# Hybrid encoder step, one core: low parts of the 128x1024 weight chunks formed by a casting and an accumulating DMA

## Chip, core and metric

The kernel runs on one NeuronCore of a Trainium2 chip. The metric is the device time of one execution, in microseconds. Three runs of the kernel before gave 2122.63, 2123.02 and 2124.85 us; the median is 2123.02 us. Five engines work side by side, each through its own queue in program order: PE (TensorE, matrix products), DVE (VectorE), ACT (ScalarE), POOL (GpSimd) and SP (SyncE, which here only issues DMAs). DMAs that POOL issues have their descriptors written by POOL itself (the software queue q0 of the profile); those of SP go through the hardware queue q1.

## What is computed

Two layers of a hybrid encoder trunk over 640 token rows (512 of a prompt, 8 x 16 of decode streams). Cut to what matters:

```python
for l in range(2):
    h = rmsnorm(x)
    a_x, a_b, a_c, dq, dk, dv, fq, fk, fv, ff, pu = split(h @ w_in[l])     # 1024 -> 2308 columns
    o_a, o_b, o_c, o_d = conv(...), diff_attn(...), fox_attn(...), pool_mix(...)
    merged = sum(sigmoid(h @ w_gate[l, i] + b) * (o_i @ w_branch[l, i]) for i in range(4))
    x = x + rmsnorm(merged @ w_out[l])
    gu = rmsnorm(x) @ w_ffn_in[l]                                          # 1024 -> 2 * 2816
    x = x + rmsnorm((silu(gu[:2816]) * gu[2816:]) @ w_ffn_out[l])
```

All of it is float32. Every matrix product is made of three products of rounded operands: each operand is split into a high part (`hi`, rounded to float32r) and a low part (`lo` = operand - `hi`), and the product is hi x hi + hi x lo + lo x hi.

## The kernel before

**Weights in chunks.** All weights come through one list, `chunks`, in the order in which they are used. A chunk is 128 rows by at most 1032 columns; its kind says how it is prepared. Kind "n" (lines 234 to 250) is the ordinary one: the chunk is loaded by SP into a tile `raw` (two buffers, line 260), and then split in halves of 512 (516) columns, the `subs`: for each half ACT copies the half into `whi` with rounding (line 295, by `copy`, line 117) and DVE subtracts it from `raw` into `wlo` (line 274, in `flush`). `whi` and `wlo` have four buffers of 516 columns each. Chunks of kind "n" with more than 512 columns are 72 in each layer: 16 of w_in and 4 of w_v, 24 of w_gate, 4 of w_out, 6 of w_ffn_in, 18 of w_ffn_out. The other kinds: "x" chunks are split as a whole into tiles that stay, "r" chunks are only loaded, and "s" parts are sums of weight blocks (the Strassen stages), which pass through the same `whi` and `wlo`; the w_branch chunks are "n" with 512 or 256 columns.

**Who drives it.** A stage asks for a half with `w_sub(key, p)` (line 310): the half is split if it was not yet, the waiting subtractions are issued (`flush`), and `w_ahead` (line 302) splits two halves more. `w_done` starts the load of the next chunk but one once a chunk's last subtraction has been issued. The order is written out by hand (`manual_schedule`): every engine's queue has the order of the Python calls, and a later instruction of an engine cannot pass an earlier one that waits.

**Stages of a layer** (times of layer 0; layer 1 follows some 1048 us later with the same shape): the first two w_in chunks in `ab_start` (line 392; to 36 us), the other chunks of the input projection in `p0` and `p1a` (lines 1367 and 1379; each chunk is 8 k-steps of 6 matmuls, `dense_k`), the gates and branches of two phases (line 1399; to 494 us) with the attention units woven in by `drive`, a Strassen stage for the last gate (to 563 us), the output projection (`mix_phase`, line 1620), `ab_start` again for the first two w_ffn_in chunks, four more of those (to 675 us), 19 Strassen steps of 7 products (line 1843, `product` at line 1831; to 913 us), and `mix_phase` for w_ffn_out.

**What the prediction's steps touch.** In `ab_start` the third chunk is asked for by `w_ahead(keys[1], 1)`, after the second half of the first chunk's products and after its evacuation:

```python
        for i in range(2):
            dense(Ds[i], w[i], x, (1,))
            evac_fn(i, Ds[i])
            if i == 0:
                w_ahead(keys[1], 1)
```

For w_in the evacuation is `ev_pu` (line 1100), which issues on POOL a memset and then the store `out_pool` (line 1111), which waits for DVE copies of the evacuated tile. POOL also carries `rstd_of` (line 338), the low parts of the attention caches (lines 746 and 758, in the decode units), the weight sums of the Strassen stages (line 451) and five small stores.

## Time and profile before

| | us |
|---|---|
| median of three runs | 2123.02 |
| span of the profiled execution | 2121.1 |
| PE busy in it | 2044.4 |
| DVE busy | 1489.7 |
| ACT busy | 983.7 |
| POOL busy | 694.6 |

The profiled execution lies 1.9 us below the median of the runs; the terms of a sum are made against its span. PE is granted its full clock nearly throughout. A busy share is an average over stages; the lists of waits say in which stage an engine stood still and for whom. A group of instructions is named by line, engine, operation and tiles (`wlo<-raw,whi`); "[2.23 <-DVE wlo L274]" behind a row of a timeline is the idle time before it and what ended it. For a DMA the issue is a row of the issuing engine, and "to landing" the time from that issue to the last byte.

### The profile page before, as it was taken

What the parts mean: (1) busy time and instruction counts of PE and PEld (TensorE: products, weight loads), DVE (VectorE), ACT (ScalarE), POOL (GpSimd) and SP (SyncE); (2) the same over time, 40 slices, a digit from 0 to 9 for tenths busy, and PEclk for the clock granted to TensorE, in tenths of its full rate; (3) what the DMA queues carried; (4) which work ended last, traced back from release to release, by engine and by line L of the source; (5) the groups of instructions that cost most, each with busy time, mean ns of one, the idle gap of its engine ahead of it and who ended that gap; (6) DMA issues with size and microseconds to landing.
All of it is one profiled execution on the core that took longest, in us unless ns stands there. A gap on an engine that the chain in (4) does not pass through costs nothing.

```text
span 2121.1 us, 34713 instructions
## 1 busy us (share of the span) xinstructions
PE 2044.4 (96%) x13050; PEld 1927.9 (91%) x13050; DVE 1489.7 (70%) x2746; ACT 983.7 (46%) x2100; POOL 694.6 (33%) x618
## 2 busy tenths in 40 slices
PE   7999999989999999999999999999899999999998
PEld 7999999988889999988899999999888899999887
DVE  5677477689768888853475774775996698888432
ACT  5556455545443433443356554565444444334431
POOL 3111055465315444400040101554751345543000
PEclk9999999999999999999999999999999999999999
DMA  4312244332251222222523122443223422222223
GB/s 146 108 61 86 72 145 138 124 123 75 94 172 60 80 81 91 89 80 75 169 75 117 57 82 82 152 149 130 83 72 115 159 75 80 80 88 67 92 97 119
DMA packets 100744, 214.35 MB, mean 101 GB/s; under 512 B 10896, under 2 KB 35056, under 8 KB 100576
## 3 DMA queue, kind: packets, MB, share of 16 engines
q1 hardware_dynamic: 99552, 209.16, 29.6%
q0 software_dynamic: 1024, 2.98, 0.4%
q8 instruction: 102, 1.67, 0.3%
q14 instruction: 66, 0.54, 0.1%
HBM read 196.02 MB, written 16.08 MB: 100 GB/s over the span
## 4 chain that ended last, share of the span: by engine, by line
PE 68%; DVE 18%; issue 6%; ACT 3%; DMA 2%; POOL 2%; SPq 0%; DVEq 0%; ACTq 0%; POOLq 0%
PE D L376 21%; PE D L1632 11%; PE S L1837 7%; DVE wlo L274 6%; PE D L1837 4%; PE O L1632 3%; PE T L1632 3%; PE D L1413 2%; DVE s L1849 2%; PE T L1837 2%; PE O L1837 2%; PE D L1274 2%; DVE s L473 1%; PE O L808 1%; ACT whi L117 1%
## 5 line engine op out<-in xcount | busy, mean ns | idle before, releaser
L274 DVE TENSOR_TENSOR wlo<-raw,whi 128x512 fp32r<-128x512 f32 (+2 forms) x388 | 294.6, 764 | 183.1 <-ACT whi L117 178.7
L117 ACT ACTIVATE whi<-raw 128x512 fp32r<-128x512 f32 (+2 forms) x390 | 230.3, 606 | 166.9 <-issue 73.8
L274 DVE TENSOR_TENSOR wlo<-s,whi 128x512 fp32r<-128x512 f32 x196 | 210.7, 1077 | 17.9 <-ACT whi L117 16.6
L117 ACT ACTIVATE s<-s 128x512 fp32r<-128x512 f32 (+7 forms) x294 | 176.3, 619 | 91.7 <-POOL s L1425 38.7
L376 PE MATMUL D<-Qh,whi 128*128 128x320 f32 (+2 forms) x736 | 177.1, 315 | 4.0 <-DVE s L1417 3.6
L376 PE MATMUL D<-Ph,whi 128*128 128x320 f32 (+2 forms) x736 | 176.8, 314 | 4.2 <-DVE s L1417 3.5
L338 POOL TENSOR_TENSOR r<-ms,mhalf 128x1 f32<-128x1 f32 x40 | 22.0, 551 | 477.1 <-DVE ms L1677 408.5
L376 PE MATMUL D<-Qh,wlo 128*128 128x320 f32 (+2 forms) x736 | 174.3, 311 | 3.8 <-DVE wlo L274 3.8
L376 PE MATMUL D<-Ph,wlo 128*128 128x320 f32 (+2 forms) x736 | 173.8, 310 | 4.3 <-DVE wlo L274 4.3
L376 PE MATMUL D<-Ql,whi 128*128 128x320 f32 (+2 forms) x736 | 173.8, 310 | 0.0
L376 PE MATMUL D<-Pl,whi 128*128 128x320 f32 (+2 forms) x736 | 173.4, 310 | 0.0
L746 POOL TENSOR_TENSOR s<-s,s 128x512 fp32r<-128x512 f32 x64 | 85.0, 1328 | 181.9 <-ACT s L117 168.9
L117 ACT ACTIVATE whi<-s 128x512 fp32r<-128x512 f32 x196 | 117.3, 621 | 36.4 <-PE S L1837 12.4
L758 POOL TENSOR_TENSOR s<-s,s 128x512 fp32r<-128x512 f32 x64 | 92.9, 1469 | 123.0 <-ACT s L117 100.9
L376 PEld LDWEIGHTS D<-Qh,whi 128*128 128x128 f32 x736 | 123.5, 190 | 6.8 <-DVE s L1417 4.4
L376 PEld LDWEIGHTS D<-Qh,wlo 128*128 128x128 f32 x736 | 125.2, 189 | 4.6 <-DVE wlo L274 4.6
L376 PEld LDWEIGHTS D<-Ph,wlo 128*128 128x128 f32 x736 | 124.5, 189 | 5.3 <-DVE wlo L274 5.3
L376 PEld LDWEIGHTS D<-Ph,whi 128*128 128x128 f32 x736 | 123.0, 189 | 7.0 <-DVE s L1417 4.0
L376 PEld LDWEIGHTS D<-Ql,whi 128*128 128x128 f32 x736 | 125.6, 189 | 0.2
L376 PEld LDWEIGHTS D<-Pl,whi 128*128 128x128 f32 x736 | 125.1, 189 | 0.6 <-DVE Pl L120 0.4
L451 POOL TENSOR_TENSOR s<-V,V 128x512 f32<-128x512 f32 x48 | 77.1, 1607 | 94.4 <-DMA V<-in_w_fi 67.0
L117 ACT ACTIVATE s<-T 128x320 fp32r<-128x320 f32 (+6 forms) x132 | 50.9, 386 | 99.1 <-PE T L520 61.5
(487 smaller groups left out, 5978.9 us busy)
## 6 DMA issues: line engine op xcount, KB each, us to landing
raw<-in_w_gate SPq DMA_DIRECT2D x48, 512.0 KB, 3.5
raw<-in_w_fi SPq DMA_DIRECT2D x48, 512.0 KB, 3.5
raw<-in_w_fo SPq DMA_DIRECT2D x44, 512.0 KB, 3.5
V<-in_w_fi SPq DMA_DIRECT2D x80, 256.0 KB, 3.0
raw<-in_w_in SPq DMA_DIRECT2D x32, 512.0 KB, 3.4
s<-in_ck_d SPq DMA_DIRECT2D x32, 256.0 KB, 4.3
s<-in_cv_d SPq DMA_DIRECT2D x32, 256.0 KB, 4.0
s<-in_ck_f SPq DMA_DIRECT2D x32, 256.0 KB, 4.1
```

The source lines that it names most:

```text
L117: A.activation(out=out, in_=in_, func=AF.Copy, scale=scale)
L274: E.tensor_tensor(out=lo, in0=raw, in1=hi, op=ALU.subtract)
L338: G.tensor_tensor(out=out, in0=ssum, in1=mhalf[:, :n], op=ALU.pow)
L376: PE.matmul(Dt[:, h, :c1 - c0], a, b[:, k, c0:c1], start=(start and pi == 0), stop=(stop and pi == 2))
L451: G.tensor_tensor(out=o[:, :512], in0=x, in1=y, op=op)
L746: G.tensor_tensor(out=lo[:, :512], in0=raw[:, :512], in1=f32(hi[:, :512]), op=ALU.subtract)
L758: G.tensor_tensor(out=lo[:, :512], in0=t[:, :512], in1=f32(hi[:, :512]), op=ALU.subtract)
L1274: PE.matmul(acc[t], x, w[:, kk, :], start=(k == 0 and pi == 0), stop=(k == 7 and pi == 2))
L1413: PE.matmul(Dt[:, h, :HT], w[:, b, k, :], x[:, 2 * br + k, h * HT:(h + 1) * HT], start=(c == 0), stop=(c == 5))
L1632: PE.matmul(ps, a, b, start=(first and pi == 0), stop=(last and pi == 2))
L1837: PE.matmul(ps[:, :HT], w, x[k], start=(k == 0 and pi == 0), stop=(k == 3 and pi == 2))
L1849: V.tensor_tensor(out=out, in0=a, in1=b, op=op)
```

## The change

Chunks of kind "n" with more than 512 columns get a kind of their own, "a", and leave the list of SP loads. Such a chunk takes a pair of tiles `whi` and `wlo` of 1032 columns (three buffers each; before, four of 516), and three steps make it: POOL issues a DMA from DRAM that casts the chunk into `whi`; ACT writes -`whi` into `wlo` (128x1024); POOL issues a second DMA from the same place in DRAM that adds the chunk onto `wlo`. The steps are moved on by `w_step`, which is called in every `w_sub` and at a few other places; an entry goes one step further per call, and all the way when the asked-for half is its own. `w_ahead` now looks at most two pairs ahead of the current one. The remaining users of `whi` and `wlo` take halves of such pairs (`w_half`). At the start, the first two chunks are asked for before the loads of x for tiles 3 and 4, and the two subtractions that POOL did there (`flush(G)`) are gone. The scratch space for POOL's DMA descriptors is set to 8192 bytes per partition.

```diff
--- before.py
+++ after.py
@@ -241,13 +241,16 @@
                 sidx[key, p] = len(subs)
                 subs.append((key, p, i, 0, 512, kind, False))
             continue
+        if kind == "n" and n > 512:
+            for p in range(2):
+                sidx[key, p] = len(subs)
+                subs.append((key, p, i, p * (n // 2), n // 2, "a", p == 1))
+            continue
         loads.append(i)
         if kind == "r":
             continue
-        parts = 2 if kind == "n" and n > 512 else 1
-        for p in range(parts):
-            sidx[key, p] = len(subs)
-            subs.append((key, p, i, p * (n // parts), n // parts, kind, p == parts - 1))
+        sidx[key, 0] = len(subs)
+        subs.append((key, 0, i, 0, n, kind, True))
     lpos = {i: n for n, i in enumerate(loads)}
     raw_t, hl_t = {}, {}
     ptr = {"dma": 0, "split": 0}
@@ -257,7 +260,7 @@
         while ptr["dma"] <= min(upto, len(loads) - 1):
             i = loads[ptr["dma"]]
             _, src, n, _ = chunks[i]
-            t = wpool.tile([128, 1032], F32, tag="raw", name=nm("raw"))
+            t = wpool.tile([128, 1024], F32, tag="raw", name=nm("raw"))
             SP.dma_start(out=t[:, :n], in_=src)
             raw_t[i] = t
             ptr["dma"] += 1
@@ -267,6 +270,9 @@
         w_dma(lpos[i] + 2)
 
     low_part = []
+    pipe = []
+    calls = [0]
+    half = []
 
     def flush(E=V):
         while low_part:
@@ -275,10 +281,41 @@
             if done:
                 done()
 
+    def w_step(j=-1):
+        calls[0] += 1
+        for e in list(pipe):
+            must = e["j"] <= j
+            if e["stage"] == 0 and (must or e["call"] < calls[0]):
+                copy(e["lo"], f32(e["hi"]), -1.0)
+                e["stage"], e["call"] = 1, calls[0]
+            if e["stage"] == 1 and (must or e["call"] < calls[0]):
+                G.dma_start(out=e["lo"], in_=e["src"], accum_op=ALU.add)
+                pipe.remove(e)
+
+    def w_pair():
+        return tuple(wpool.tile([128, 1032], F32R, tag=t, bufs=3, name=nm(t)) for t in ("whi", "wlo"))
+
+    def w_half():
+        if not half:
+            pair = w_pair()
+            half.extend([[t[:, c:c + 512] for t in pair] for c in (0, 512)])
+        return half.pop(0)
+
     def w_split(upto):
         while ptr["split"] <= min(upto, len(subs) - 1):
             j = ptr["split"]
             key, p, i, off, n, kind, end = subs[j]
+            ptr["split"] += 1
+            if kind == "a":
+                if p == 0:
+                    half.clear()
+                    hi, lo = w_pair()
+                    src = chunks[i][1]
+                    G.dma_start(out=hi[:, :2 * n], in_=src)
+                    pipe.append({"j": j, "hi": hi[:, :2 * n], "lo": lo[:, :2 * n], "src": src, "stage": 0, "call": calls[0]})
+                    for q in range(2):
+                        hl_t[j + q] = (hi[:, q * n:(q + 1) * n], lo[:, q * n:(q + 1) * n])
+                continue
             if kind == "s":
                 src, done = ext[key[0]](key, p)
             else:
@@ -292,25 +329,36 @@
                 flush()
                 w_done(i)
             else:
-                hi = wpool.tile([128, 516], F32R, tag="whi", bufs=4, name=nm("whi"))
-                lo = wpool.tile([128, 516], F32R, tag="wlo", bufs=4, name=nm("wlo"))
+                hi, lo = w_half()
                 copy(hi[:, :n], src)
                 low_part.append((lo[:, :n], src, f32(hi[:, :n]), done))
                 hl_t[j] = (hi, lo)
-            ptr["split"] += 1
 
     def w_ahead(key, p, n=2):
         j = sidx[key, p]
-        while n > 0 and j + 1 < len(subs):
+        pairs, room, j0 = 0, len(half), j
+        while j + 1 < len(subs):
+            kind, part = subs[j + 1][5], subs[j + 1][1]
+            if kind == "a":
+                new, left = (1, 0) if part == 0 else (0, 0)
+            elif kind == "x":
+                new, left = (0, room) if pairs < 2 else (1, 0)
+            else:
+                if j + 1 - j0 > n:
+                    break
+                new, left = (0, room - 1) if room else (1, 1)
+            pairs += new
+            if pairs > 2:
+                break
+            room = left
             j += 1
-            if subs[j][5] != "x":
-                n -= 1
         w_split(j)
 
     def w_sub(key, p=0, ahead=2):
         j = sidx[key, p]
         w_split(j)
         flush()
+        w_step(j)
         w = hl_t.pop(j)
         if ahead:
             w_ahead(key, p, ahead)
@@ -424,9 +472,8 @@
     def vtile(i):
         return hpool.tile([128, 512], F32, tag=f"V{i}", name=nm("V"))
 
-    w_dma(0)
+    w_split(3)
     x_first.append(load_x(I["x"], 3))
-    w_dma(1)
     x_first.append(load_x(I["x"], 4))
     tabD = const("tabD", C_D, 512)
     tabDD = const("tabDD", C_DD, KEYS)
@@ -1700,6 +1747,8 @@
             for t in range(5):
                 for n, k in enumerate(ks):
                     mm(acc[t], t, k, S.win[k], k == 0, k == nk - 1)
+                    if n % 4 == 1:
+                        w_step()
                     if n == 3 and t == 1 and nx:
                         w_split(sidx[nx[1], 1])
                         flush()
@@ -1944,11 +1993,11 @@
 
             normed(0)
             normed(1)
+            w_step()
             turned(0)
             normed(2)
+            w_step()
             turned(1)
-            w_split(1)
-            flush(G)
             turned(2)
             normed(3)
 
@@ -2078,7 +2127,7 @@
     from concourse.bass_utils import run_bass_kernel_spmd
 
     arrays = _pack({k: np.asarray(v) for k, v in inputs.items()})
-    nc = bacc.Bacc("TRN2", target_bir_lowering=False, num_devices=1)
+    nc = bacc.Bacc("TRN2", target_bir_lowering=False, num_devices=1, dynamic_dma_scratch_size=8192)
     ins, outs, feed = {}, {}, {}
     for n, v in arrays.items():
         feed[f"in_{n}"] = v
```

## Rows read from the trace of the kernel before

**Rows 1.** Page: the chain that ended last, share of the span by engine

```profile
PE 68%; DVE 18%; issue 6%; ACT 3%; DMA 2%; POOL 2%; SPq 0%; DVEq 0%; ACTq 0%; POOLq 0%
```

**Rows 2.** Waits of PE: line waited for whom, us in total, times, longest

```profile
PE S L361 <- DVE s L353: 14.0, 4, 9.5
PE O L808 <- DVE s L793: 10.0, 4, 3.7
...
PE D L376 <- DVE wlo L274: 8.1, 7, 2.3
PE D L376 <- DVE s L1417: 7.1, 4, 2.2
...
PE O L1274 <- DVE wlo L274: 3.9, 2, 2.1
```

**Rows 3.** Groups by line and form: busy us, mean ns, idle before

```profile
L274 DVE TENSOR_TENSOR wlo<-raw,whi 128x512 fp32r<-128x512 f32 x340 | 254.6, 754 | 180.2 <-ACT whi L117 176.1 <-PE D L376 3.8
...
L117 ACT ACTIVATE whi<-raw 128x512 fp32r<-128x512 f32 x342 | 208.3, 624 | 166.8 <-issue 73.8 <-PE D L1632 33.1 <-DMA raw<-in_w_fo 27.1
```

**Rows 4.** Instructions on tile raw: duration min/median/max ns, first and last start

```profile
L117 ACT ACTIVATE Ph<-raw x4: 1059/1060/1062, 569.9 to 584.6; 128x1024 fp32r<-128x1024 f32 x4
```

**Rows 5.** DMA issues by line (KB, us to landing), then line L1203's issues and landings

```profile
raw<-in_w_fi SPq DMA_DIRECT2D x48, 512.0 KB, 3.5
...
out_fk<-s POOLq DMA_DIRECT2D x4, 320.0 KB, 3.5
...
L1203 POOL DMA_DIRECT2D out_fk<-s x4: 540/541/542, 161.7 to 1227.9; - x4
...
DMA to landing us min/median/max: 2.4/3.4/5.0
```

**Rows 6.** Line L1304, POOL's slowest DMA issue

```profile
L1304 POOL DMA_DIRECT2D out_lf<-lf x2: 923/925/927, 90.6 to 1138.9; - x2
```

**Rows 7.** Timelines, third w_in chunk of layer 0: start us, us, engine

```profile
34.99 0.74 POOL L1111 DMA_DIRECT2D out_pool<-s  x1 [10.24 <-DVE s L1110]
...
36.27 0.45 PE L376 MATMUL D<-Ph,whi 128*128 128x320 f32 x2
...
40.62 0.42 ACT L117 ACTIVATE s<-s 128x256 fp32r<-128x256 f32 x1 [2.25 <-DMA s<-in_pool_w]
```

**Rows 8.** Timeline of POOL, the same place in layer 1

```profile
1083.24 0.61 POOL L1111 DMA_DIRECT2D out_pool<-s  x1 [9.20 <-DVE s L1110]
```

**Rows 9.** Timeline of PE, last Strassen products into w_ffn_out

```profile
908.05 0.31 PE L1837 MATMUL D<-Qh,whi 128*128 128x320 f32 x1
...
913.32 0.40 PE L1632 MATMUL O<-whi,s 128*128 128x512 f32 x1
913.56 0.40 PE L1632 MATMUL O<-wlo,s 128*128 128x512 f32 x1
```

**Rows 10.** Timeline of PE, into the output projection

```profile
563.59 0.39 PE L1632 MATMUL O<-whi,s 128*128 128x512 f32 x1
565.17 0.50 PE L1632 MATMUL O<-wlo,s 128*128 128x512 f32 x1 [1.19 <-DVE wlo L274]
```

**Rows 11.** Timelines, third w_ffn_in chunk: ACT, then PE

```profile
638.43 0.77 ACT L1772 ACTIVATE s<-D 128x384 f32<-128x384 f32 x2 [2.04 <-PE D L376]
...
641.98 0.45 PE L376 MATMUL D<-Qh,whi 128*128 128x320 f32 x2
...
654.63 0.56 PE L376 MATMUL D<-Qh,wlo 128*128 128x320 f32 x2 [2.23 <-DVE wlo L274]
```

**Rows 12.** Timeline of POOL in the decode units

```profile
394.25 3.00 POOL L758 TENSOR_TENSOR s<-s,s 128x512 fp32r<-128x512 f32 x2 [9.18 <-ACT s L117]
```

**Rows 13.** Start: timeline of DVE; stages by engine, clock, DMA share, GB/s

```profile
8.59 1.41 DVE L353 SCALAR_TENSOR_TENSOR s<-s,r,s 128x512 f32<-128x512 f32 x2 [3.11 <-DMA s<-in_g_norm]
...
0.00:20.00 20.00, 7.50 (x28) 6.10 (x29) 8.57 (x15) 11.12 (x24) 4.53 (x11) 1.00 0.74 260
...
130.00:217.00 87.00, 87.00 (x636) 86.61 (x636) 66.30 (x201) 52.01 (x132) 9.20 (x9) 1.00 0.22 75
```

## Prediction

> **What bounds the kernel now.** First the page: PE is busy for 2044.4 of 2121.1 us, so at most some 77 us can be won by any change that leaves the products as they are; this change does. The chain that ended last [rows 1] runs over PE for 68% and over DVE for 18%: the reader sees that PE is the bound, and that DVE is the one engine that often holds it up. Then the list of PE's own waits [rows 2], which says where. The 14.0 us on L361 are transposes that wait for the normalised x; no weight is in that chain. The waits that DVE's load can cause are 8.1 us (weights' low parts in the dense chunks), 7.1 (a branch's gating, which frees a psD buffer), 10.0 (the decode units' product with V) and 3.9 (the v unit), 29.1 us in all. From 130 to 217 us PE is busy for all of 87.0 us [rows 13]: there, no faster split is worth anything. So the prize is 29 us at most, and the question is what the new way of making a chunk costs in delay: the old one had its data on chip two chunks early, the new one has a chain of two DMAs with a step of ACT between them.
>
> **Part by part.**
>
> *Removed.* 144 chunks, so 288 subtractions on DVE of 754 ns [rows 3], 217 us of its 1490, and 288 copies on ACT of 624 ns [rows 3], 180 us. All of this lies beside PE's work; only through the waits of [rows 2] is any of it on the path. In the stages in question (gates with decode units) I take half of the 10.0 and 7.1 us as gone, because those chains also hold other DVE and POOL steps, so -8.5. Of the 8.1 us, 2.2 us in each layer are those of the first w_ffn_in chunks [rows 11], dealt with below; the other 3.6 go. Together **-12 us**, bounds 0 and -25.
>
> *Added on ACT.* 144 copies of 128x1024 at 1.06 us [rows 4], 153 us: ACT has less to do than before. But ACT now waits for a casting DMA inside its queue, with evacuations behind it. It is called half a chunk after the DMA, and a chunk takes 48 products or 24 pairs; with 87 us for 636 products [rows 13] that is 6.6 us and more. So it comes some 3.5 us after a DMA that takes about 4, a delay of half a microsecond on an engine that is half idle: 0.
>
> *Added on POOL.* 288 DMA issues of 0.54 us [rows 5], 156 us on an engine busy for 695 of 2121. Nothing of it is on the path by itself. But each second DMA stands in POOL's queue behind whatever POOL waits for, and each first DMA waits for PE to leave a pair, with all later POOL work behind it (in the decode units the low parts of the caches, which the scores need).
>
> *Length of the chain.* No casting or adding DMA is in the trace. The nearest rows: POOL's 320 KB stores land 3.4 us after the issue (2.4 to 5.0), SP's loads of 512 KB after 3.5 [rows 5]. For a 512 KB cast I take 3.8 us, for the adding one, which must read two streams, 4.2; bounds 2.4 and 7.0 (twice a plain load). The chain is then 3.8 + 1.06 + 4.2 = 9.1 us, with hand-overs. The Trainium skill (DMA: Bandwidth & Descriptors, "Anatomy of one DMA — SWDGE (gpsimd) path") fits a POOL-issued DMA as 2.0 us and bytes over 436e3 per us; as an estimate from it 512 KB would be 3.2 us, each chain 1.6 us shorter and the whole sum some 9 us lower. The stores of [rows 5] at 320 KB and 3.4 us lie above that fit, so the row is used.
>
> *Steady state.* Where one "a" chunk follows another, the cast is issued two chunks ahead (13 us and more) and the adding one a chunk ahead: 9.1 us fit, 0. Where branches lie between (gates), the lead of the adding DMA is the branch alone: 12 to 24 products, 1.8 to 3.5 us without the attention in between, when POOL's queue is up to date only then. In the decode part POOL's waits end on ACT and then work 3.0 us [rows 12]. For the 16 chunks of the second gate phase I take 0.5 us each, **+8**; bounds 0 and 3 us each (48), as POOL is late or early.
>
> *Cold starts.* These are the terms I am surest of, since they follow from the program's order. Before, the raw tile was there and only a copy and a subtraction stood between `w_ahead` and the products.
> In `ab_start` for w_in the third chunk is asked for after the first chunk's evacuation, and on POOL that evacuation ends with `out_pool`, from 34.99 to 35.73 us [rows 7]. Behind it the cast: landed at 35.7 + 3.8 = 39.5. ACT is held by the copy of pool_w until 41.04 [rows 7], then 1.06: 42.1. The adding DMA lands at 46.3. PE comes to this chunk at 36.27 [rows 7] and after four products, 0.6 us, needs the low part: it waits 9.4 us. In layer 1 `out_pool` ends at 1083.85 [rows 8], at the same point of the stage. Against this the 3.9 us of the v unit's waits [rows 2], for a low part that DVE no longer makes, go. 2 x 9.4 - 3.9 = **+15**; bounds 2 x 4 - 4 and 2 x 12.
> Into w_ffn_out: `w_ahead` reaches the first chunk three products ahead, at 908.05; PE takes it up at 913.32 and wants the low part at 913.56 [rows 9]. 908.05 + 3.8 + 1.06 + 4.2 = 917.1: 3.6 us in each layer, **+7**; before there is no wait there. Into w_out: the same lead of 5.3 us (the last product and two branches) before 563.59 [rows 10]: 563.6 - 5.3 + 9.1 = 567.4, wanted at 563.8, 3.6 less the 1.19 of now [rows 10], **+5** for both. Bounds of the two: 0 and 18. In w_ffn_in the cast can go early, ACT is free at 639.2 [rows 11], so 639.2 + 1.06 + 4.2 = 644.5 against 642.6, 1.9 us; in exchange the 2.23 us [rows 11] go: 0.
> The very start: 1 MB of weights is now issued before or beside x and g_norm. DVE's first scaling waited for g_norm until 8.59, and DMA moved 260 GB/s [rows 13]; 1 MB at that rate is 4 us, **+3**, bounds 0 and 5. The two subtractions that POOL did there hid nothing that is needed sooner.
>
> *Rest.* A descriptor area of half the size, tile halves and the prefetch of raw tiles that now serves fewer loads: 0; the raw loads that remain can only come earlier.
>
> Sum: -12 + 8 + 15 + 7 + 5 + 3 = +26 us on 2121.1, so 2147; with the 1.9 us by which the median lies above the profiled span, **2149 us**.
>
> **Rivals.**
>
> *The chain is hidden, DVE's relief counts (faster).* If POOL's DMAs land in little over 2.4 us [rows 5] and POOL runs ahead of PE, starts cost 8 in all, the gates nothing, and the waits go by 25: 2123 + 8 + 3 - 25 = 2109, at best 2102. For it: POOL is idle for two thirds, DVE gives up a seventh of its work. Against it: the third chunk stands behind `out_pool` whatever the DMA takes. It decides at a chain of some 5 us instead of 9.
>
> *The adding DMA is slow.* If a DMA that computes takes 7 us and more to land, the second gate phase pays 3 us for each of its 16 chunks, the first 2 us for each of its 32, and the eight starts 6 us more each: 2149 + 40 + 64 + 48 = 2301. For it: two reads and a write for each byte, and no row that shows one. Against it: the lead of a whole chunk in the projections still holds, and DMA is busy for a third only.
>
> *Descriptors late.* In the trace the issues take 0.54 us, the slowest 0.93 [rows 5, 6]; if all 288 took the 0.93 us, the chain would be 0.8 us longer, which adds 0.8 at eight starts and 16 gates, 19 us: 2168. The Trainium skill (SBUF — State Buffer, 'The "DVE blocks DMA" trap (SWDGE)') says that POOL cannot write descriptors while a DVE instruction holds the port pair that the two share, and speaks against moving loads to POOL. By the rows that price is 0.4 us an issue at most, so the rule gets little weight.
>
> *It changes nothing.* Starts and relief might cancel: 2119 to 2127.
>
> **How the numbers follow.** The forecast, a loss of 4 to 70 us, has 0.54; the hidden chain 0.24; the slow adding DMA 0.08; late descriptors 0.04; no change 0.10. A difference of 0.2%, 4 us, is about what a measurement of this kernel can tell from none. So faster 0.24, same 0.10, slower 0.66. The forecast's own range: all costs at their lower bounds and the relief of 25 give 2121 + 4 - 25 = 2100, all costs at their upper ones and no relief 2121 + 48 + 20 + 18 + 5 = 2212. The range of 8 in 10 reaches into the faster rival and leaves out its best part and most of the slow one: 2104 to 2212.
>
> **What would show it.** Right: a wait of PE on L376 of some 9 us at about 37 us and again 1048 us later, ended by a DMA into `wlo`; waits of 3 to 4 us at the first products of w_out and w_ffn_out; DVE busy near 1270 us; fewer waits on DVE at L808 and L1413's neighbours. Wrong: landings of the adding DMA at 3 us or at 7; no wait at 37 us, which would mean that the cast is not held by `out_pool`; waits of PE spread over all chunks, which would mean that the DMA engines and not the starts are the cause; POOL's cache splits late in the decode units.

## The result and the profile after

The changed kernel takes 2481.77 us (median of four runs, 2472.88 to 2482.88) against 2123.20 us of the kernel before in the same comparison: a ratio of 1.168, 95% interval 1.166 to 1.170. The sign was forecast, the size was not: 358 us lost instead of 26.

The page of the changed kernel, first its busy times, then the granted clock of TensorE in 40 slices, then the DMA queues:

```profile
PE 2148.5 (87%) x13050; PEld 2000.5 (81%) x13050; DVE 1308.5 (53%) x2460; ACT 954.2 (38%) x1956; POOL 874.8 (35%) x904
...
PEclk9999998888989999999999999888889899999999
...
q0 software_dynamic: 42496, 154.06, 26.8%
q1 hardware_dynamic: 78816, 133.62, 16.3%
```

The span is 2479.4 us. PE's idle time grew from 2121.1 - 2044.4 = 77 us to 2479.4 - 2148.5 = 331 us, by 254. The remaining 104 us are *busy* time: the same 13050 products took longer. Most of it is the clock: by the trace's clock records PE worked 211 us at the lower of its two levels, granted 0.50, against 23 us before, and half of that difference is 94 us. The two gate stages were granted 0.88, against 0.99 before. DVE lost 181 us of work (to 1308.5 us, where some 1270 were forecast), and the span gained nothing by it.

The waits of PE in the changed kernel (line waited for whom, us in total, times, longest):

```profile
PE D L424 <- DMA wlo<-in_w_gate: 139.8, 29, 12.4
PE O L1679 <- DMA wlo<-in_w_fo: 28.9, 20, 4.7
PE D L424 <- DMA wlo<-in_w_in: 27.2, 8, 5.5
PE O L1679 <- DMA wlo<-in_w_out: 14.3, 3, 6.8
...
PE D L424 <- DMA wlo<-in_w_fi: 10.5, 2, 6.1
...
PE D L424 <- DMA whi<-in_w_in: 7.9, 2, 4.2
```

Against [rows 2], where no wait on a weight was longer than 8.1 us in sum, the reader sees one name at the top, the low part of w_gate, and the same low part for every other weight. What the three steps cost is in the instructions of the adding DMA (L292) and of the casting one (L314): duration of the issue in ns (min/median/max), and the time from issue to landing.

```profile
L292 POOL DMA_DIRECT2D wlo<-in_w_gate x48: 832/873/937, 218.9 to 1826.0; - x48
...
DMA to landing us min/median/max: 5.0/5.6/8.9
```
```profile
L314 POOL DMA_DIRECT2D whi<-in_w_gate x48: 543/612/907, 207.6 to 1811.1; - x48
L314 POOL DMA_DIRECT2D whi<-in_w_fo x36: 554/866/894, 1061.8 to 2425.4; - x36
...
DMA to landing us min/median/max: 3.7/6.3/10.1
```

Of the 144 casts, 93 go into the queue within 1.3 us behind the adding DMA of a chunk before; these land after 6.8 us in the median, the other 51 after 4.5. The chain is 6.3 + 1.06 + 5.6 = 13 us, where the prediction had 9.1. Pairing each cast with its own adding DMA in the trace, the median from the one's issue to the other's landing is 13.3 us in w_ffn_out, 14.4 in w_in and 18.3 in the gates: there something more than the length is added.

The timeline of the first gate phases, layer 0 (start, duration, idle time before and its releaser), shows where the second and third step stand:

```profile
483.71 0.58 POOL L314 DMA_DIRECT2D whi<-in_w_gate  x1
...
491.12 0.90 ACT L117 ACTIVATE s<-O 32x64 f32<-32x64 f32 x4 [9.35 <-PE O L855]
...
492.04 1.06 ACT L117 ACTIVATE wlo<-whi 128x1024 fp32r<-128x1024 f32 x1
...
494.19 0.46 PE L424 MATMUL D<-Pl,whi 128*128 128x320 f32 x2
...
494.48 0.47 PE L424 MATMUL D<-Ph,wlo 128*128 128x320 f32 x2
...
495.35 2.54 POOL L805 TENSOR_TENSOR s<-s,s 128x512 fp32r<-128x512 f32 x2 [11.05 <-ACT s L117]
...
501.53 1.26 POOL L793 TENSOR_TENSOR s<-s,s 128x512 fp32r<-128x512 f32 x1
...
503.22 0.89 POOL L292 DMA_DIRECT2D wlo<-in_w_gate  x1
...
512.06 0.90 PE L424 MATMUL D<-Ph,wlo 128*128 128x320 f32 x2 [12.36 <-DMA wlo<-in_w_gate]
512.76 0.73 PE L424 MATMUL D<-Ph,whi 128*128 128x320 f32 x2
513.29 0.73 PE L424 MATMUL D<-Pl,whi 128*128 128x320 f32 x2
```

The negation was done at 493.1. The adding DMA was issued ten microseconds later, behind the low parts of the attention caches (L805, L793) in GpSimd's queue; L805 had waited 11.05 us for ScalarE, and ScalarE 9.35 us for a product of PE (L855) that stands behind the dense products in PE's queue. PE waits for the low part, the low part for GpSimd, GpSimd for ScalarE, ScalarE for PE: a loop in which each round can pay its wait again. That is a reading of this one stretch, the longest wait of the run: the adding DMA went out 3.5 us after PE had run out of work and took 8.8 us to land, where the median is 5.6. e8 below tests the link through GpSimd.

After the wait a pair of products comes every 0.53 us (512.76, 513.29); before it, the same kind of pair came every 0.29 (494.19, 494.48). The granted clock (the column behind POOL's) of the two stretches:

```profile
490.50:503.50 13.00, 9.20 (x66) 8.68 (x65) 6.05 (x17) 6.81 (x16) 6.82 (x9) 1.00 0.07 18
...
504.00:517.00 13.00, 4.94 (x18) 4.95 (x19) 0.00 (x0) 0.00 (x0) 0.67 (x2) 0.50 0.77 223
```

So this wait was followed by products at the lower of the two levels, 1.2 instead of 2.4 GHz, and cost more than its own length. From 480 to 540 us the granted clock was 0.80 in the mean, with PE busy for 38.8 of the 60 us.

### The profile page after: what moved, and what is told of

The parts are those of the page before. It is cut to its first block, busy times and chain, and to the rows that moved or that the text cites. A ratio compares the mean times of both kernels' runs of the same rounds, so it can differ in the third digit from the quotient of the medians.

```text
span 2479.4 us, 34360 instructions
## 1 busy us (share of the span) xinstructions
PE 2148.5 (87%) x13050; PEld 2000.5 (81%) x13050; DVE 1308.5 (53%) x2460; ACT 954.2 (38%) x1956; POOL 874.8 (35%) x904
## 3 DMA queue, kind: packets, MB, share of 16 engines
q1 hardware_dynamic: 78816, 133.62, 16.3%
## 5 line engine op out<-in xcount | busy, mean ns | idle before, releaser
L117 ACT ACTIVATE wlo<-whi 128x1024 fp32r<-128x1024 f32 (+1 forms) x144 | 152.1, 1057 | 556.4 <-issue 142.3
L424 PE MATMUL D<-Ph,wlo 128*128 128x320 f32 (+2 forms) x736 | 188.7, 333 | 91.5 <-DMA wlo<-in_w_gate 71.7
L424 PE MATMUL D<-Qh,wlo 128*128 128x320 f32 (+2 forms) x736 | 186.7, 330 | 86.2 <-DMA wlo<-in_w_gate 68.1
L424 PEld LDWEIGHTS D<-Ph,wlo 128*128 128x128 f32 x736 | 134.1, 204 | 97.7 <-DMA wlo<-in_w_gate 75.7
L424 PE MATMUL D<-Ph,whi 128*128 128x320 f32 (+2 forms) x736 | 186.6, 329 | 8.1 <-DMA whi<-in_w_in 4.2
L424 PE MATMUL D<-Qh,whi 128*128 128x320 f32 (+2 forms) x736 | 185.9, 329 | 7.4 <-DMA whi<-in_w_in 3.7
L424 PE MATMUL D<-Pl,whi 128*128 128x320 f32 (+2 forms) x736 | 182.1, 323 | 0.0
L805 POOL TENSOR_TENSOR s<-s,s 128x512 fp32r<-128x512 f32 x64 | 86.7, 1379 | 184.4 <-ACT s L117 166.8
L424 PEld LDWEIGHTS D<-Ph,whi 128*128 128x128 f32 x736 | 132.4, 203 | 11.3 <-issue 4.4
L793 POOL TENSOR_TENSOR s<-s,s 128x512 fp32r<-128x512 f32 x64 | 87.6, 1369 | 105.7 <-issue 61.7
L292 POOL DMA_DIRECT2D wlo<-in_w_fo x36 | 31.1, 863 | 234.4 <-ACT wlo L117 226.5
L280 DVE TENSOR_TENSOR wlo<-raw,whi 128x512 fp32r<-128x512 f32 (+1 forms) x102 | 81.2, 796 | 36.7 <-ACT whi L117 34.5
```

The source lines that it names most:

```text
L117: A.activation(out=out, in_=in_, func=AF.Copy, scale=scale)
L280: E.tensor_tensor(out=lo, in0=raw, in1=hi, op=ALU.subtract)
L292: G.dma_start(out=e["lo"], in_=e["src"], accum_op=ALU.add)
L424: PE.matmul(Dt[:, h, :c1 - c0], a, b[:, k, c0:c1], start=(start and pi == 0), stop=(stop and pi == 2))
L793: G.tensor_tensor(out=lo[:, :512], in0=raw[:, :512], in1=f32(hi[:, :512]), op=ALU.subtract)
L805: G.tensor_tensor(out=lo[:, :512], in0=t[:, :512], in1=f32(hi[:, :512]), op=ALU.subtract)
```

## The experiments

Stage times below are worked out from the trace: from a stage's first product to the next stage's first, both layers added, in us. "V, attention" runs from 50 to 217 us in layer 0 of the kernel before (its second half is the last stretch of [rows 13]); "gates" are the first two phases, from 217 to 491 us. The two Strassen stages are left out; they grew by 11 us together in the changed kernel.

| stage | before | changed | e4 | e8 | e16 | e14 | e13 |
|---|---|---|---|---|---|---|---|
| w_in, first two and third chunk | 62 | 86 | 85 | 88 | 82 | 85 | 62 |
| V, attention | 335 | 386 | 357 | 392 | 358 | 327 | 335 |
| gates | 548 | 721 | 666 | 558 | 541 | 535 | 530 |
| w_out | 125 | 153 | 143 | 150 | 142 | 136 | 123 |
| w_ffn_in | 95 | 108 | 103 | 106 | 103 | 103 | 96 |
| w_ffn_out | 308 | 364 | 320 | 363 | 320 | 323 | 308 |
| median of the runs | 2123 | 2482 | 2335 | 2326 | 2205 | 2160 | 2106 |

Theories: the *queues* (the second and third step stand behind work that waits for PE); the *length* (the chain is longer than its lead); the *bytes* (the software queue or the DMA engines are too slow wherever they are used); the *clock* as a cause of its own.

**Where it is lost.** e1 gives the gates' chunks back to the old way, e2 changes them alone:

```
-        if kind == "n" and n > 512:
+        if kind == "n" and n > 512 and key[0] != "g":     # e1;  == "g" in e2
```

> The 48 w_gate chunks go back to SyncE load, ScalarE high part and VectorE low part; the other 96 chunks stay with the casting and the adding DMA. Theory of the lead (the three steps take about 13 us against a lead of at most two chunks, 13.7 us, and in the gate phases the second and third step also stand in ScalarE's and GpSimd's queues behind attention work): the loss is local, the two gate stages return from 362 and 359 us to about 274 each, 2482 - 173 = 2309 us (2290 to 2330). Rival, the software queue is too slow for its bytes wherever it is used: every chunk loses the same 358 / 144 = 2.5 us, so 2482 - 119 = 2363 us, and the gate stages keep part of their excess. Rival, the lower TensorE clock is no consequence of the waits: the gate stages stay near a clock of 0.86 and about 40 us of their excess remains.

> The complement: only the 48 w_gate chunks are made by the casting and the adding DMA, all others as in the kernel before. Lead theory: 2123 + 173 = 2296 us (2275 to 2315), the gate stages at about 360 each and all others as before. Rival of equal loss by bytes: 2123 + 119 = 2242 us. If the stages disturb one another (one stage's transfers delay the next), the two halves do not add up: this run's excess and that of its complement together miss 358 us by more than 30.

Measured: e1 2297.9 us (ratio 1.081, 1.076 to 1.087), gate stages of 276 and 278 us; e2 2314.1 us (1.089, 1.084 to 1.094), gate stages of 360 and 359, the others as before but for w_out (13 us more). The two excesses, 173 and 189, add up to 362 us, against 358 in the changed kernel: the loss is local to the stages. By bytes the gates would have lost a third of it, and they lose half. In e1 the gates run nearly as before and are granted 0.98 of the clock, against 0.88 in the changed kernel, so the low clock was no cause of its own.

**One part alone, and one property taken away.** e3 keeps the cast and makes the low part on VectorE from a raw tile that SyncE loads beside it. e4 takes only the accumulating out (the low part then misses its subtraction):

```
-                copy(e["lo"], f32(e["hi"]), -1.0)                             # e3
...
-                G.dma_start(out=e["lo"], in_=e["src"], accum_op=ALU.add)
...
+                V.tensor_tensor(out=e["lo"][:, c], in0=raw_t[e["i"]][:, c], in1=f32(e["hi"][:, c]), op=ALU.subtract)
...
-                G.dma_start(out=e["lo"], in_=e["src"], accum_op=ALU.add)      # e4
+                G.dma_start(out=e["lo"], in_=e["src"])
```

> One half of the change alone: the high part is made by the casting DMA; the low part is again a VectorE subtraction, from a raw tile that SyncE loads beside it (the same number of bytes is moved as in the changed kernel, half of it by the hardware queue). The negating copy and the adding DMA are gone. Lead theory: the casting DMA no longer stands behind an adding DMA and lands in about 4 us, the subtractions take 1.5 us more, the chain falls from 13 to about 6 us, and nearly all of the 358 us goes: 2125 to 2180 us. Rival, the casting DMA itself or the doubled traffic is what costs: above 2300 us, with high parts that still land after 6 us.

> The third step is a plain casting DMA that writes the chunk over the negated copy instead of adding to it (so the low part's subtraction is left out); queues, order and bytes are the same. If accumulating is the dear thing, its landing falls from 5.6 us towards 4 and the cast queued behind it from 6.3 towards 5, the chain from 13 to about 10.5 us, and the time to 2250 to 2330 us. If what costs is the queue and its order, the landing stays within 0.5 us and the time between 2430 and 2490 us.

Measured: e3 2197.9 us (1.034, 1.031 to 1.037), 18 us above the expected range, high parts landing in 3.9 to 4.9 us (medians by weight); the rest of its loss is again at starts (w_in 40 and 38 us, w_ffn_in 56 in each layer instead of 48) and 12 us in each gate stage. e4 2334.9 us (1.099, 1.096 to 1.102), 5 us above its range. In e4 the third step has the same place, queue and bytes, and its issue and landing are:

```profile
L292 POOL DMA_DIRECT2D wlo<-in_w_gate x48: 527/567/617, 203.3 to 1711.3; - x48
...
DMA to landing us min/median/max: 3.6/3.9/7.6
```
```profile
L314 POOL DMA_DIRECT2D whi<-in_w_fo x36: 527/537/577, 1006.0 to 2279.5; - x36
...
DMA to landing us min/median/max: 3.6/4.7/8.8
```

So accumulating makes this DMA land 1.7 us later (5.6 against 3.9), its issue 0.3 us longer, and the cast behind it 1.6 us later (6.3 against 4.7), with an issue of 0.54 again instead of 0.87 us. The chain is 4.7 + 1.06 + 3.9 = 9.7 us, nearly the one predicted (cast to landing, 9.9 us in the median in w_ffn_out), and 147 us are back. But 212 us of loss remain, 118 of them in the gates, where cast to landing still takes 16.3 us: the length alone was not the error.

**The queues.** e5 negates on VectorE. e8 moves the attention caches' 128 subtractions from GpSimd to VectorE; in the changed kernel GpSimd is idle for 290 us before them, and ScalarE ends 211 of these (the 272 us of the expectation are neither). e9 does both.

```
-                copy(e["lo"], f32(e["hi"]), -1.0)                                            # e5
+                V.tensor_scalar(out=e["lo"], in0=f32(e["hi"]), scalar1=-1.0, scalar2=None, op0=ALU.mult)
...
-                G.tensor_tensor(out=lo[:, :512], in0=t[:, :512], in1=f32(hi[:, :512]), op=ALU.subtract)   # e8
+                V.tensor_tensor(out=lo[:, :512], in0=t[:, :512], in1=f32(hi[:, :512]), op=ALU.subtract)
```

> Only the engine of the second step is changed: VectorE negates the high part in place of ScalarE. Theory of the queues (in the gate stages the second step stands behind ScalarE's evacuation s<-O, which waits 9 to 19 us for TensorE, while TensorE waits for the low part): the gate stages fall from 362 and 359 us by some 15 to 40 each, the whole to 2400 to 2455 us. Theory of the length (only the 13 us of the three steps count, wherever they queue): 2465 to 2490 us, since the copy takes about 1 us on either engine.

> The attention cache's low parts (128 subtractions of 1.37 us on GpSimd, lines 793 and 805) move to VectorE, so that GpSimd, which issues the casting and the adding DMA, no longer waits in them for ScalarE (272 us of idle time stands before them in the changed kernel). Theory of the queues: the adding DMA is issued earlier in the gate stages, which fall by 15 to 40 us each; 2400 to 2455 us. Theory of the length: no change, 2465 to 2490 us. If VectorE's queue becomes a wait of its own, the time rises above 2490 us.

> Both moves together: the negation and the attention cache's subtractions on VectorE. Theory of the queues: the second and the third step are each freed only if both are (the adding DMA follows the negation), so that the two together give more than the sum of the two alone: gate stages of 290 to 320 us, 2340 to 2400 us in all. Theory of the length: 2460 to 2490 us.

Measured: e5 2457.6 us (1.157), between the ranges of the two theories, gates unchanged at 362 and 360; its 24 us come from V, attention (17) and w_ffn_out (9). e8 2325.7 us (1.095, 1.091 to 1.099), far more than expected, all of it in the gates (280 and 279 us). e9 2321.9 us (1.093), less than either theory had: against e8, what the negation's move gains in V, attention (19) and w_ffn_out (6) it loses for the most part in the gates (14, now 287 and 285). PE's waits in e8:

```profile
PE D L424 <- DMA wlo<-in_w_in: 27.0, 8, 5.8
PE O L1679 <- DMA wlo<-in_w_fo: 26.4, 19, 4.7
PE D L424 <- DMA wlo<-in_w_gate: 23.6, 15, 3.9
```

w_gate's row fell from 139.8 to 23.6 us while the other two stayed. In the gates, from the end of the negation to the issue of its adding DMA, the changed kernel takes 4.0 us in the mean, e5 4.2 and e8 1.0; the whole chain falls from 18.3 us in the median to 14.0 in e8. So it did not matter which engine negates, and it mattered what stands ahead of the adding DMA on GpSimd. (The cache copies for which those subtractions wait stayed on ScalarE in every run; that link of the loop was not taken out by itself.) The adding DMA itself still took 5.7 us to land there, and the same bytes were moved, so neither the DMA engines nor the bytes held up the gates. The control e13 moves the same subtractions in the kernel before:

> A control: the kernel before with the attention cache's 128 subtractions on VectorE and nothing else. If the gain of moving them in the changed kernel comes from the adding DMA behind them, there is none here, where no weight passes GpSimd's queue: 2115 to 2135 us, the gate stages at 270 to 280. If the subtractions were slow on GpSimd for TensorE in any case, the time falls by 20 us or more.

Measured: 2106.5 us against 2126.3 (0.990, 0.988 to 0.992), gates of 265 us each. The expectation missed: the move is worth some 20 us without any weight on GpSimd. Of e8's 156 us, 136 are thus the change's, if the two add up: the place behind those subtractions. e13 is also the fastest kernel of the study.

**The length.** e7 gives the chain one chunk more of lead (four tiles for the high part; `if pairs > 3`, negation two half chunks after the cast). e10 adds the move of e8, e11 also the early request of w_in's third chunk.

> One chunk more of lead: four tiles for the high part instead of three, the casting DMA asked for three chunks ahead instead of two, the negation two half chunks after it instead of one, the adding DMA as before half a chunk after the negation; the space comes from the buffer that GpSimd's descriptors are written to (4096 instead of 8192 bytes a partition). The lead grows from 13.7 to 20.5 us. If the loss is a chain longer than its lead, by its own length or by queues, most of it goes in the steady stages: gate stages of 280 to 300 us, w_ffn_out near 160, in all 2200 to 2280 us, with the waits at the start of each stage left. If the bytes of the software queue or TensorE's clock set the time, it stays above 2400 us.

> Both remedies together: the attention cache's subtractions on VectorE, and one chunk more of lead (four tiles for the high part, the negation two half chunks after the cast). If the loss has two separate parts, the adding DMA queued behind GpSimd's waiting subtractions in the gate stages, and a chain longer than its lead everywhere else, their gains add up: 2482 - 156 (the first alone) - 105 (the second's own gain outside the gate stages: 30 + 30 in the attention and V stages, 21 + 17 in w_ffn_out, 8 + 7 in w_out, some 8 elsewhere, less 16 lost at the two starts of w_in) = 2221 us, and the gate stages stay at 270 to 280 us: 2195 to 2235 us in all. If one cause is behind both, the second adds little: 2280 to 2325 us.

> As the run before it, and in the first two accumulations of a w_in and w_ffn_in stage the third chunk is asked for with the second, ahead of the matmuls, instead of after the first evacuation; its negation and its adding DMA stand behind the first chunk's and the second chunk's first halves. The prediction put 9.4 us of wait at the third chunk of each w_in stage on that late request. If that is its cause, the two w_in stages fall by 8 to 20 us each, to 32 to 40 us, and the whole by 16 to 40 us against the run before it (2181 to 2205 us if that one is at 2221). If the wait is one for bandwidth at the stage's start, the stages stay.

Measured: e7 2435.7 us (1.147), e10 2364.0 (1.111), e11 2348.7 (1.104), 15 us less than e10 where 16 to 40 were expected; the starts of w_in fell from 101 to 88 us. Both expectations for e7 and e10 missed, and the place is plain: V, attention fell to 326 us and w_ffn_out to 327, as the theory of the length has it, but the gates rose to 780 (e7) and stayed at 708 us (e10). The timeline of e10 shows why:

```profile
474.66 1.04 ACT L117 ACTIVATE wlo<-whi 128x1024 fp32r<-128x1024 f32 x1
476.00 0.85 POOL L293 DMA_DIRECT2D wlo<-in_w_gate  x1 [6.50 <-ACT whi L117]
476.55 0.87 POOL L315 DMA_DIRECT2D whi<-in_w_gate  x1
...
481.61 0.63 PE L428 MATMUL D<-Ph,wlo 128*128 128x320 f32 x1 [6.77 <-DMA wlo<-in_w_gate]
```

The branch chunk takes a tile pair of the ring and ends the look-ahead, so the lead in the gates was no longer than before, while I had put the negation half a chunk later: it ended at 475.7 us, 0.9 us after PE had run out of work, and PE waited out the adding DMA. That was a fault of the experiment, not of the theory. e14 asks for the negation as soon as its tile is free and looks past the branch chunk; e15 adds the early request:

```
-            if e["stage"] == 0 and (must or e["call"] < calls[0]):
+            if e["stage"] == 0 and (must or e["call"] < calls[0] and e["pn"] - cur[0] <= 2):
...
+                w_split(sidx[keys[1], 1] + 1)          # e15: in ab_start, ahead of the first matmuls
```

> Again both remedies together, without what the run of the two before it got wrong: the negation is asked for half a chunk after the cast wherever its tile is free (there it came two half chunks later, in the gate stages only just ahead of its use, because the branch chunk takes part in the ring and kept the lead at two). Now the branch chunk may be passed as well, four tiles for the high part, three for the low part. If the two parts of the loss are separate, the gate stages are at 280 us or less as with the moved subtractions alone, the other stages as with the longer lead (163, 164, 70 us), the start of w_in as in the changed kernel: 2482 - 156 - 120 = 2206 us (2190 to 2240). If they are one, 2280 to 2325 us.

> As the run before it, with the third chunk of w_in and w_ffn_in asked for ahead of the first matmuls. If the late request is what the start of w_in waits for, the two w_in stages fall from about 44 and 41 us to 34 to 38, and the whole by 10 to 25 us against the run before it. If not, they stay.

> The attention cache's subtractions on VectorE, lead as in the changed kernel, and a plain casting DMA in place of the adding one (the low part's subtraction is left out). With GpSimd's queue free, what is left is the length of the chain: about 9.5 us here, which is the length that the prediction took, against 13. If my prediction failed by this length and by the queue alone, the stages outside the gates fall as they did without accumulation (V and attention 177 to 180, w_ffn_out 157 to 162, w_out 71) and the gate stages to 272 to 278 us: 2326 - 100 = 2226 us (2205 to 2245), of which the late requests at the stages' starts are then the largest part.

Measured: e14 2160.2 us (1.017, 1.012 to 1.023), below the 2190 that the theory of separate causes gave as its lowest, since the gates too gained from the lead (267 us each); e15 2160.7 (1.018, 1.014 to 1.021); e16 2205.4 (1.039, 1.035 to 1.043), at the lower end of its range. The two remedies together take back 322 of the 358 us (20 of these e13 has too): 156 with the moved subtractions, a further 166 from e8 to e14. The longer lead alone, without the fault of e7, was not run. With the plain third step instead of the lead the four cases are there: e4 gives back 147 us, e8 156, both together (e16) 276, so the causes are separate for the most part; they overlap in the gates, where the plain step gives 55 us with the subtractions ahead of it and 17 without. PE's waits of e14:

```profile
PE O L1690 <- DMA wlo<-in_w_out: 16.0, 4, 6.9
...
PE O L1690 <- DMA wlo<-in_w_fo: 10.1, 3, 4.1
PE D L434 <- DMA wlo<-in_w_in: 9.9, 3, 5.4
PE D L434 <- DMA wlo<-in_w_fi: 9.8, 2, 5.2
...
PE D L434 <- DMA wlo<-in_w_gate: 3.8, 3, 1.5
```

w_gate is gone from the top, and what is left are mostly single waits at the stages' starts, which this lead did not cover. e16, with GpSimd free and the plain third step, still has 23 us in V, attention and 12 in w_ffn_out over e13: the chain of 9.7 us did not fit into its lead either. e15 did not win anything in sum, where 10 to 25 us were expected: w_in's starts fell from 85 to 80 us, and V, attention rose from 327 to 333. Its GpSimd queue at the start of layer 0:

```profile
23.97 0.60 POOL L318 DMA_DIRECT2D whi<-in_w_in  x1
...
37.90 0.61 POOL L1175 DMA_DIRECT2D out_pool<-s  x1 [11.54 <-DVE s L1168]
38.51 0.54 POOL L318 DMA_DIRECT2D whi<-in_w_in  x1
39.03 0.55 POOL L318 DMA_DIRECT2D whi<-in_w_v  x1
39.55 0.94 POOL L293 DMA_DIRECT2D wlo<-in_w_in  x1
```

The cast went out at 23.97 us (40.44 in e14) and the negation was done at 34.1 (46.9), but the adding DMA stood behind `out_pool` and two casts until 39.55 (47.15), and PE waited 7.69 us for it.

**Only where it runs steadily.** e12 (with e10's fault), e17 and e18 (with e14's remedies) use the change in w_v and w_in from the fifth chunk on; e12 and e18 in w_gate too.

> The same two remedies, but casting and adding DMAs only where a stage runs steadily: the chunks of w_gate, w_v and w_in from the fifth on; the chunks of w_out, w_ffn_in, w_ffn_out and the first four of w_in are loaded and split as in the kernel before. If the cold starts and w_ffn_out carry what is left, the stages w_in, w_out, w_ffn_in and w_ffn_out stand as in the kernel before, the attention and V stages 4 us under it each (163 instead of 167 us, as with the longer lead), the gate stages at 270 to 280: 2123 - 8 + 0 to 10 = 2110 to 2130 us. If the gate stages still wait for the adding DMA: 2130 to 2160 us.

> The kernel before with the attention cache's subtractions on VectorE (2106 us alone), and casting and adding DMAs, with the longer lead, for the chunks of w_v and of w_in from the fifth on alone. With both remedies the V and attention stages took 163.5 us against 167.4 without the change, so if the prediction's term of removed work (it put 12 us, hidden behind nothing) is real, each layer gains 3 to 4 us there: 2098 to 2102 us, the lowest of all. If the first changed chunk after an unchanged one waits for its chain (some 5 us a layer), 2106 to 2114 us.

> As the run beside it, and the w_gate chunks too, which with both remedies took 267.5 us a layer against 265.0 without the change: 4 to 6 us more than the run beside it, 2100 to 2120 us. If the gate stages come out under 265 us, the change pays there and this is the lowest.

Measured: e12 2323.9 us (1.093, 1.091 to 1.095), e17 2153.0 (1.014, 1.012 to 1.016), e18 2149.0 (1.011, 1.010 to 1.013). None reaches e13, and all three lie above what was expected (e18 was to lie 4 to 6 us above e17). In e17 each layer's first changed chunk waits for nearly its whole chain:

```profile
PE O L1334 <- DMA wlo<-in_w_v: 24.1, 2, 12.2
```

Without those 12 us its V, attention stages (177 us) would lie 2 to 3 us under the 167 of e13: a gain seems to be there, and each entry into the new way costs several times as much. These waits are 24 of the 46 us by which e17 lies above e13. Another 13 stand in the gates (543 against 530) and 13 in w_out (136 against 123), though e17 makes the chunks of both in the old way; w_out is as long in e2, e12 and e18 (135 to 137), where its chunks are also the old ones. What these kernels share there with the changed one is above all the ring of tile pairs and the look-ahead; no run changes these alone, so the cause is not shown.

## Why the prediction was wrong, point by point

- **Direction: right; mechanism: in part.** The chain of three steps lands late and DVE's relief does not pay for it. But what carries most of the loss, a queue priced at 8 us, was missed. Stage by stage, first what the sum had and then what the trace shows: the very start +3 and +2; w_in +19 and +24; V, attention -4 (the v unit's waits) and +51; gates about 0 (+8 for the queue, -8.5 of removed waits) and +173; w_out +5 and +28; w_ffn_in 0 and +12; w_ffn_out +7 and +57; the Strassen stages 0 and +11.
- **"Length of the chain", 9.1 us: mis-sized.** 13 us. The negation was right (1.06). The adding DMA took 5.6 us for my 4.2, and the cast 6.3 for my 3.8; I priced each alone, not two in one queue. Of the cast's 2.5 us more, 1.6 go when the DMA ahead does not accumulate (e4); the other 0.9 were not separated. e4 puts the share of accumulating at 147 us, e16 against e8 at 120. The Trainium skill (DMA: Bandwidth & Descriptors, "Anatomy of one DMA — SWDGE (gpsimd) path") would give 3.2 us for 512 KB as an estimate; a plain casting DMA took 3.9 in e4, an adding one 5.6, so the rows decide, and its line says nothing of accumulating.
- **"Steady state", 0 where one changed chunk follows another: the step that failed outside the gates.** I set a lead of "13 us and more" against 9.1. Against 13 (14.4 in w_in) it leaves nothing for hand-overs and queues: V, attention lost 51 us and w_ffn_out 57. Even the 9.7 us of e16 did not fit. With one chunk more of lead (e14) V, attention is 8 us *faster* than before.
- **"Added on POOL" and the +8 for the gates: the step that failed most.** The prediction named the queue ("each second DMA stands in POOL's queue behind whatever POOL waits for") and then priced POOL's work of 3.0 us in [rows 12] and not the 9.18 us of wait beside it, which is what a DMA behind it inherits; and only for the second phase. The whole of that wait stood in the trace of the kernel before, 305 us of idle time ahead of its 128 subtractions, 270 of it ended by ScalarE:

```profile
L746 POOL TENSOR_TENSOR s<-s,s 128x512 fp32r<-128x512 f32 x64 | 85.0, 1328 | 181.9 <-ACT s L117 168.9
...
L758 POOL TENSOR_TENSOR s<-s,s 128x512 fp32r<-128x512 f32 x64 | 92.9, 1469 | 123.0 <-ACT s L117 100.9
```

  The gates lost 173 us, and moving the subtractions off POOL gave 156 back (136 beyond what the same move gives the kernel before). I did not see that the wait can close a loop over ScalarE and PE and so repeat.
- **"Cold starts": right at w_in, short at the others.** At w_in's third chunk PE waited 4.22 us for the high and 5.51 us for the low part, 9.7 against 9.4 predicted, behind `out_pool` as stated; in layer 1 3.7 and 5.0. w_out's first wait was 6.8 instead of 3.6 (its adding DMA took 8.1 us to land), w_ffn_out's 4.6 instead of 3.6: the longer chain. In w_ffn_in, put at 0, PE waited 4.3 and 6.1 us for the low part. The starts are most of the 54 us by which e14 still stands above e13.
- **"Removed", -12: not where it was put.** The waits of the decode units were to give 8.5 us back in the gates; e14's gates lie 5 us above e13's. V, attention is 8 us shorter in e14 than before, 3.9 of them the v unit's waits of [rows 2], which the sum had under the cold starts. In the changed kernel none of this shows.
- **"Rest", 0: in part wrong.** w_out is 10 to 13 us longer even where its own chunks are made in the old way and only the ring of tile pairs and the look-ahead are new (e2, e12, e17, e18). Which part of the rearrangement costs this stays open.
- **Left out: the clock.** 104 us of longer products came with 254 us of idle time, 94 of them by the lower level.
- **Rivals.** "The adding DMA is slow" was the right name with a wrong threshold: 5.6 us were enough, and its 2301 us counted neither the queue nor the clock. Waits of PE "spread over all chunks" were to mean that the DMA engines are the cause; they were spread over the chunks of w_gate and w_ffn_out, and e8, with the same bytes, shows another cause in the gates. "Descriptors late": issues did take 0.87 us, but in e4, where only the accumulating is gone, they took 0.53 to 0.59 (medians by weight) again with VectorE as busy (1311 us). The rule of the Trainium skill (SBUF — State Buffer, 'The "DVE blocks DMA" trap (SWDGE)') is thus not what lengthened them here.
- **Open:** why the move of e13 helps the kernel before by 20 us was not followed further.

## What to carry to other kernels

When a DMA moves to a queue that a computing engine issues, look first at the *idle* column of that engine's rows: the DMA inherits every wait ahead of it, and if that wait leads back to the engine that needs the data, it can repeat at each round. Chain the steps with their queueing, not each alone, and compare the chain with the lead at every entry into a stage as well as in its middle. Then try the cheap rearrangement by itself: here moving 128 subtractions off GpSimd gave 20 us, while the change's own gain, where a run let it show (V, attention in e14), was 8.

## What the runs showed of the hardware

- Accumulating into SBUF cost a 512 KB DMA 1.7 us of landing (5.6 against 3.9) and 0.3 us of issue (0.87 against 0.57), and the cast in the same queue 1.6 us of landing (6.3 against 4.7), by the medians of the changed kernel and of e4.
- A casting DMA of GpSimd without an adding one in its queue landed in 3.9 to 4.9 us (e3, medians by weight), SyncE's plain load of the same bytes in 3.5 [rows 5].
- After a wait of 12.4 us the products ran at the lower clock level, granted 0.50 from 504 to 517 us; from 480 to 540 us it was 0.80 in the mean, with PE busy for 38.8 of the 60 us.
